# Modulation rows by matmuls of 32 columns, with the squares and scalings spread between them

## The chip, the cores and the metric

The kernel runs on one core of a Trainium2 chip. The metric is the device time of one execution in microseconds (us). The engines named below are PE (the matrix engine, TensorE), PEld (its weight loads, shown apart), DVE (VectorE), ACT (ScalarE), POOL (GpSimd) and SP (SyncE, which here issues the DMAs).

## The reference, cut to what matters

One layer of a diffusion backbone: a short gated convolution and a bidirectional mLSTM side by side, then a gated feed-forward network. There are 128 context tokens and 2048 latent tokens of width 1024, all in float32. The shift, scale and gate vectors of each normalisation come from a conditioning vector, one for the context and one for the latent tokens:

```python
mod_ctx = (jax.nn.silu(c_ctx) @ w_mod[l] + b_mod[l])[None, None, :]
mod_lat = (jax.nn.silu(c) @ w_mod[l] + b_mod[l])[:, None, :]
...
shift1, scale1, gate1, shift2, scale2, gate2 = jnp.split(mod, 6, axis=-1)
h = rmsnorm(x, norm1) * (1 + scale1) + shift1
z = h @ w_in                                    # conv parts, q, k, v, o, mLSTM gates
...
h_m, C, n, m = mlstm_bidir(heads(q), heads(k), heads(v), gates, C0, n0, m0)
...
x = x + gate1 * (jnp.concatenate([y_sc, h_m], axis=-1) @ w_out)
h2 = rmsnorm(x, norm2) * (1 + scale2) + shift2
up = conv3((h2 @ w_up).reshape(B, rows, row_len, 2 * D_FF), conv_ffn_w, conv_ffn_b, axis=ffn_axis)
a, gg = jnp.split(up.reshape(B, T, 2 * D_FF), 2, axis=-1)
x = x + gate2 * ((jax.nn.silu(gg) * a) @ w_down)
```

`mod` has 6 x 1024 entries for each of the two conditioning vectors. In blocks of 128 these are 48 modulation rows of the kernel (16 of them are `shift1` and `scale1`).

## The kernel before, in words

Tokens stand along the free axis, channels on the 128 partitions (8 tiles of 128 channels). Nothing can be multiplied by `w_in` before the input is normalised, scaled and shifted, so the kernel opens with the following, in `hymba_kernel`:

- `mod_pe(mt)` computes one modulation row. SP loads a tile of `w_mod` of 128 x 1024 (512 KB) into one of six buffers (`wsu` twice, `xg` four times, by `homes6`). Eight float32 matmuls (L628) accumulate over the 8 channel tiles. Their stationary operand is the weight block of 128 x 128; the moving operand `csil` has two distinct columns (context and latent), repeated by a broadcast to 128. DVE then adds the bias (L630) and writes the two columns that matter into `modT`.
- `mods(k0, k1)` runs rows 8+k (scale) and k (shift) for each k and then `affine` (L120), which makes the combined scale `ab`. The 16 rows are called w0 to w15 below, in this order.
- `gsquares` squares the 8 input tiles of the first 512 tokens on ACT and adds them on DVE (L590). `inv_rms` sums over partitions by four matmuls of one column (L129), scales on DVE (L132) and takes the power on POOL (L133). `spread` broadcasts the result to all partitions by four matmuls (L140).
- `gapply` multiplies each input tile (L600) and adds the shift; `put` (L594, L595) splits the result into a rounded high part `hH` and a low part `hL`. Float32 products are done as three matmuls of such parts.
- `vg_of(0)`, by `vg` (L397 to L404), then computes values and gates for the first block: 8 groups of 24 matmuls of 264 columns, each group ended by a write-out on ACT (L402) and an addition on DVE (L404). `second()` prepares the next block meanwhile.

The other 32 modulation rows aren't needed until late. `mod_dve` (the function around L896) computes them on DVE: for each row one load of 512 KB and two multiply-and-sum instructions over 128 x 1024 (half-rows). It is a generator called `side`. Its steps are called from three places: `vg_first` (values and gates of the blocks after those), the gate phase, and the weave of the mLSTM sums. The gate phase (`gate_phase`) computes the log forget gates on DVE and ACT (`fe`, `fc`), which PE transposes (L964).

The program is written through a scheduling layer that sets each engine's order from the order of the code, with its own view of costs and of free buffers; so an instruction may stand elsewhere on its engine than in the code.

Of the kernel before, what the change touches and what calls it, by code (L numbers as in the profile page):

```python
# [10 lines left out]
F32 = mybir.dt.float32  # L11
F32R = mybir.dt.float32r
AF = mybir.ActivationFunctionType
# [5 lines left out]
P = 128  # L19
# [24 lines left out]
def bc(ap, shape):  # L44
    return ap.to_broadcast(shape)
# [13 lines left out]
def hymba_kernel(ctx: ExitStack, tc: tile.TileContext, I, O):  # L59
    nc = tc.nc  # L60
    V, S, G, PE, Q = nc.vector, nc.scalar, nc.gpsimd, nc.tensor, nc.sync
# [30 lines left out]
    csil = cst.tile([P, KT, 2], F32, name="csil")  # L92
# [8 lines left out]
    ssp = ctx.enter_context(tc.tile_pool(name="ssp", bufs=2))  # L101

    def run(g, side=None, every=1):
        for i, _ in enumerate(g):
            if side and i % every == 0:
                next(side, None)
# [11 lines left out]
    def affine(n, k0, k1):  # L118
        s0 = 8 if n == 0 else 32
        V.scalar_tensor_tensor(ab[:, n, k0:k1], modT[:, s0 + k0:s0 + k1, :], 1.0,  # L120
                               bc(nrm[:, n, k0:k1, None], [P, k1 - k0, 2]), op0=ALU.add, op1=ALU.mult)

    def inv_rms(ss, n, r):

        nch = (n + P - 1) // P
        ps = pst.tile([P, 512], F32, name="st")
        for i in range(nch):
            w = min(P, n - i * P)
            PE.matmul(ps[:w, i:i + 1], ss[:, i * P:i * P + w], ones[:, 0:1], start=True, stop=True)  # L129
        for i0, i1, w in ((0, n // P, P), (n // P, nch, n % P)):  # L130
            if i0 < i1 and w:
                V.tensor_scalar(r[:w, i0:i1], ps[:w, i0:i1], 1.0 / D, EPS, op0=ALU.mult, op1=ALU.add)  # L132
                G.tensor_tensor(r[:w, i0:i1], r[:w, i0:i1], mhalf[:w, i0:i1], op=ALU.pow)  # L133

    def spread(r, n):

        ps = pst.tile([P, 512], F32, name="st")
        for i in range((n + P - 1) // P):
            w = min(P, n - i * P)
            PE.matmul(ps[:, i * P:i * P + w], bc(r[:w, i:i + 1], [w, P]), ident[:w, :w], start=True, stop=True)  # L140
        return ps
# [63 lines left out]
    def accumulator():  # L205
        pool = pa[next(turn_a) % len(pa)]
        return pool.tile([P, 512], F32, name="acc")
# [157 lines left out]
    with ExitStack() as ph1:  # L365
# [4 lines left out]
        sqp = ph1.enter_context(tc.tile_pool(name="sqp", bufs=2))  # L370
# [14 lines left out]
        def load_vg(j):  # L385
            return [load_w(I["w_vg"][j, kk], WN) for kk in range(2)]
# [163 lines left out]
        with tc.tile_pool(name="ex", bufs=1, side="right") as ex, \  # L550
# [16 lines left out]
            def raws(blk):  # L567
                def get(pool, name, k0, n, bufs):
                    t = pool.tile([P, 4, 384] if n > 2 else [P, 2, NG], F32, name=name, bufs=bufs)
                    t = t.rearrange("p k t -> p (k t)")[:, :n * NG].rearrange("p (k t) -> p k t", t=NG)  # L570
                    Q.dma_start(t, I["x"][k0:k0 + n, :, TG + blk * NG:TG + (blk + 1) * NG].rearrange("k p t -> p k t"))
                    return [t[:, i] for i in range(n)]

                if blk == 0:
                    return get(xp, "xt", 0, 3, 2) + get(xp, "xt", 3, 3, 2) + get(xg, "xh", 6, 2, 1)
                return [x for k in range(0, KT, 2) for x in get(xg, "xg", k, 2, 4)]

            def gcol(blk):
                c = TG // P + 4 * blk
                return rc[:, c:c + 4]  # L580

            def gsquares(xr):
                ss = ssp.tile([P, 512], F32, name="ss")
                for k, x in enumerate(xr):
                    if k == 0:
                        S.activation(ss, x, AF.Square)
                        continue
                    sq = sqp.tile([P, 512], F32, name="sq")
                    S.activation(sq, x, AF.Square)
                    V.tensor_add(ss, ss, sq)  # L590
                return ss

            def put(x, to):
                S.activation(to[0], x, AF.Copy)  # L594
                V.tensor_sub(to[1], x, to[0].bitcast(F32))  # L595

            def gapply(blk, xr):
                rb = spread(gcol(blk), NG)
                for k, x in enumerate(xr):
                    V.scalar_tensor_tensor(x, x, ab[:, 0, k, 1:2], rb[:, :NG], op0=ALU.mult, op1=ALU.mult)  # L600
                    S.activation(x, x, AF.Identity, bias=modT[:, k, 1:2])
                    put(x, plain[blk][k])
                    yield

            def gsums(x1, x2):
                for kk in range(4):
                    b11, b21, b12, b22 = x1[kk], x1[kk + 4], x2[kk], x2[kk + 4]
                    V.tensor_sub(b11, b12, b11)
                    put(b11, gs[0][kk])
                    V.tensor_sub(b12, b22, b12)  # L610
                    yield
                    V.tensor_sub(b22, b22, b11)
                    put(b22, gs[1][kk])
                    V.tensor_sub(b21, b21, b22)
                    put(b12, gs[2][kk])
                    yield
# [3 lines left out]
            def mod_pe(mt):  # L620
                if next(homes6) == "u":
                    st = ex.tile([P, WN], F32, name="wsu", bufs=2)
                else:
                    st = xg.tile([P, 2, NG], F32, name="xg", bufs=4).rearrange("p k t -> p (k t)")
                Q.dma_start(st[:, :D], I["w_mod"][mt])
                ps = accumulator()
                for k in range(KT):
                    PE.matmul(ps[:, :P], st[:, k * P:(k + 1) * P], bc(csil[:, k, None, :], [P, 64, 2]),  # L628
                              start=(k == 0), stop=(k == KT - 1))
                V.tensor_scalar(modT[:, mt, :], ps[:, :2], bmod[:, mt:mt + 1], None, op0=ALU.add)  # L630

            def mods(k0, k1):
                for k in range(k0, k1):
                    mod_pe(8 + k)
                    mod_pe(k)
                    affine(0, k, k + 1)
# [6 lines left out]
            Q.dma_start(ident, I["ident"])  # L643
            mods(1, 2)
            x1 = raws(0)
            ss = gsquares(x1)
            mods(2, 4)
            ws = load_vg(0)
            inv_rms(ss, NG, gcol(0))
            mods(4, 8)  # L650
            run(gapply(0, x1))
            ws += load_vg(1)
            Q.dma_start(bgate, I["b_gate"].to_broadcast([P, 16]))
            x2 = raws(1)

            def second():
                ss = gsquares(x2)
                yield
                inv_rms(ss, NG, gcol(1))
                yield  # L660
                yield from gapply(1, x2)
# [5 lines left out]
            side = second()  # L667
# [6 lines left out]
            side = gsums(x1, x2)  # L674
# [187 lines left out]
            side = chain(first_stats(), prep_down())  # L862
# [39 lines left out]
        side = mod_dve()  # L902
# [277 lines left out]
        def weave(units, fill, blocks, lead, side=None):  # L1180

            n = len(units)
            for i in range(-1, n + 3):
                if 0 <= i < n:
                    units[i].first()
                if 0 <= i - 3 < n:
                    units[i - 3].third()
                if 0 <= i - 1 < n:
                    units[i - 1].second()
                for x in range(lead) if i < 0 else (i + lead,):  # L1190
                    if x < n:
                        units[x].load()
                for _ in range(blocks[i % 3]):
                    next(fill, None)
                if side and i % 2:
                    next(side, None)


        def vg_first():
            for b in BA:  # L1200
                hH, hL = hs[b]
                yield from vg(chunks(b), lambda k: (hH[:, k], hL[:, k]), ws, rq)

        for x, _ in enumerate(vg_first()):
            next(third, None)
            if x % 2:
                next(side, None)
        run(third)
        with tc.tile_pool(name="gt", bufs=1, side="right") as gt:
            gph = gate_phase()  # L1210
            kh = heads(BA, hs, 16, kD, AF.Copy, 1.0)
            while True:
                try:
                    next(gph)
                except StopIteration as e:
                    cols, colc, decB = e.value
                    break
                run(islice(kh, 2), side, 2)
            run(kh, side, 2)
        sbs, sfs = [], []  # L1220
        for hp in range(2):
            sb = ml.tile([P, 2, 2, 129], F32, name="sb", bufs=5)
# [31 lines left out]
        side = sums(0, fpool, (0,), (6,))  # L1254
# [16 lines left out]
    with ph2:  # L1271
# [141 lines left out]
        side = sums(1, fpool)  # L1413
# [77 lines left out]
        for w, (hf, x) in enumerate(PRODS):  # L1491
            n = HN[hf] // 2 // NP[hf]
            for mp, ps in units_of(w):
                acc = {p: bank(next(turn))[:, :n] for p in ps}
                for c, nk in enumerate(KS):
# [4 lines left out]
                    for p in ps:  # L1500
                        for kk in range(nk):
                            k = slice(kk * P, (kk + 1) * P)
# [9 lines left out]
                    if jobs and jobs[0][0] + 1 <= step:  # L1512
                        k, ch = jobs[0]
# [93 lines left out]
```

## Time and profile before

| quantity | value |
|---|---|
| median of 3 runs | 2476.62 us (2476.61 to 2480.12) |
| the profiled execution, in all | 2481.01 us |
| its span in the profile | 2479.2 us |
| mean granted clock of PE | 0.991 |
| PE / PEld / DVE / ACT busy | 98% / 94% / 73% / 46% |
| PE's idle time before the first modulation row | 5.6 us |
| PE's idle time before the fifth row | 3.3 us |
| PE's idle time before the first matmul of `vg_of(0)` | 2.6 us |
| PE's idle time before L964 (gate phase) | 3.4 us |

Durations are read from the profiled execution and held against its own span; the median of the runs is what is compared between kernels. PE is busy nearly always, so the places that matter are those at which it stands idle or runs at a lower granted clock. The profile gives the granted clock for any stretch of time; a share of 0.50 means half of full speed.

### The profile page before, as it was taken

What the parts mean: (1) busy time and instruction counts of PE and PEld (TensorE: products, weight loads), DVE (VectorE), ACT (ScalarE), POOL (GpSimd) and SP (SyncE); (2) the same over time, 40 slices, a digit from 0 to 9 for tenths busy, and PEclk for the clock granted to TensorE, in tenths of its full rate; (3) what the DMA queues carried; (4) which work ended last, traced back from release to release, by engine and by line L of the source; (5) the groups of instructions that cost most, each with busy time, mean ns of one, the idle gap of its engine ahead of it and who ended that gap; (6) DMA issues with size and microseconds to landing.
All of it is one profiled execution on the core that took longest, in us unless ns stands there. A gap on an engine that the chain in (4) does not pass through costs nothing.

```text
span 2479.2 us, 42907 instructions
## 1 busy us (share of the span) xinstructions
PE 2427.5 (98%) x16347; PEld 2322.7 (94%) x16347; DVE 1806.6 (73%) x3419; ACT 1146.3 (46%) x2166; POOL 65.4 (3%) x127
## 2 busy tenths in 40 slices
PE   8999999999999999999999999999999999999998
PEld 7987889989999989999999999999999988889998
DVE  4767678862567776888798879776767787677665
ACT  4533453352344444465454446555545554543343
POOL 0000000000101110000000000000000000000000
PEclk9999999999999999999999999999999999999999
DMA  7457557787567886966465446544444486576444
GB/s 287 129 191 256 206 191 223 234 257 217 163 190 232 280 249 197 302 233 234 143 229 195 164 143 240 185 149 161 138 161 145 164 292 221 201 275 208 173 155 149
DMA packets 249119, 506.08 MB, mean 204 GB/s; under 512 B 22722, under 2 KB 143698, under 8 KB 238034
## 3 DMA queue, kind: packets, MB, share of 16 engines
q1 hardware_dynamic: 248914, 503.35, 61.0%
q8 instruction: 128, 2.10, 0.4%
q14 instruction: 77, 0.63, 0.1%
HBM read 355.24 MB, written 148.03 MB: 203 GB/s over the span
## 4 chain that ended last, share of the span: by engine, by line
PE 78%; DMA 11%; DVE 7%; issue 2%; ACT 1%; SPq 1%; POOL 0%; DVEq 0%; ACTq 0%; POOLq 0%
PE pa L1446 7%; PE pa L1448 7%; PE pa L1447 7%; PE acc L216 4%; PE acc L218 4%; PE acc L217 4%; PE pb L1448 3%; PE pb L1446 3%; PE pb L1447 3%; PE pa L1505 2%; PE pa L1504 2%; PE pa L1506 2%; PE pc L1446 2%; PE pc L1448 2%; PE pc L1447 2%; DMA wm<-in_w_modr 2%
## 5 line engine op out<-in xcount | busy, mean ns | idle before, releaser
L1446 PE MATMUL pa<-tH,wh 128*128 128x272 f32 x1408 | 409.1, 291 | 3.1 <-DVE row L502 2.3
L1448 PE MATMUL pa<-tH,wl 128*128 128x272 f32 x1408 | 408.3, 290 | 0.0
L1447 PE MATMUL pa<-tL,wh 128*128 128x272 f32 x1408 | 406.3, 289 | 0.3 <-DVE tL L283 0.3
L289 ACT ACTIVATE wh<-st 128x512 fp32r<-128x512 f32 (+1 forms) x312 | 189.5, 609 | 412.8 <-PE pa L1447 117.2
L216 PE MATMUL acc<-hH,wh 128*128 128x384 f32 (+1 forms) x960 | 330.4, 344 | 0.0
L218 PE MATMUL acc<-hH,wl 128*128 128x384 f32 (+1 forms) x960 | 322.0, 335 | 0.0
L217 PE MATMUL acc<-hL,wh 128*128 128x384 f32 (+1 forms) x960 | 321.2, 335 | 0.0
L1287 DVE SCALAR_TENSOR_TENSOR tt<-raw,fw,tt 128x127 f32<-128x127 f32 (+4 forms) x264 | 242.3, 948 | 43.5 <-ACT tt L1293 42.3
L290 DVE TENSOR_TENSOR wl<-st,wh 128x512 fp32r<-128x512 f32 (+1 forms) x312 | 205.4, 661 | 92.8 <-ACT wh L289 88.9
L1446 PEld LDWEIGHTS pa<-tH,wh 128*128 128x128 f32 x1408 | 265.9, 189 | 3.9 <-DVE row L502 2.4
L1447 PEld LDWEIGHTS pa<-tL,wh 128*128 128x128 f32 x1408 | 266.7, 189 | 0.5 <-DVE tL L283 0.5
L1448 PEld LDWEIGHTS pa<-tH,wl 128*128 128x128 f32 x1408 | 265.6, 189 | 0.0
L1446 PE MATMUL pb<-tH,wh 128*128 128x272 f32 x704 | 204.0, 290 | 1.9 <-ACT tH L282 1.1
L1448 PE MATMUL pb<-tH,wl 128*128 128x272 f32 x704 | 203.8, 290 | 0.0
L1447 PE MATMUL pb<-tL,wh 128*128 128x272 f32 x704 | 202.9, 288 | 0.0
L216 PEld LDWEIGHTS acc<-hH,wh 128*128 128x128 f32 x960 | 182.0, 190 | 1.4 <-issue 0.4
L217 PEld LDWEIGHTS acc<-hL,wh 128*128 128x128 f32 x960 | 181.7, 189 | 0.8
L218 PEld LDWEIGHTS acc<-hH,wl 128*128 128x128 f32 x960 | 181.5, 189 | 0.4 <-issue 0.2
L289 ACT ACTIVATE wh<-s 128x512 fp32r<-128x512 f32 x176 | 110.9, 630 | 150.5 <-PE pc L1447 90.5
L290 DVE TENSOR_TENSOR wl<-s,wh 128x512 fp32r<-128x512 f32 x176 | 120.8, 687 | 32.1 <-ACT wh L289 28.3
L1446 PEld LDWEIGHTS pb<-tH,wh 128*128 128x128 f32 x704 | 132.6, 188 | 2.5 <-ACT tH L282 1.3
L1447 PEld LDWEIGHTS pb<-tL,wh 128*128 128x128 f32 x704 | 132.9, 189 | 0.1
(301 smaller groups left out, 5931.9 us busy)
## 6 DMA issues: line engine op xcount, KB each, us to landing
st<-in_w_up SPq DMA_DIRECT2D x88, 512.0 KB, 4.7
wU<-s SPq DMA_DIRECT2D x22, 1024.0 KB, 7.6
s<-wU SPq DMA_DIRECT2D x22, 1024.0 KB, 5.5
st<-wD SPq DMA_DIRECT2D x32, 704.0 KB, 4.2
st<-in_w_down SPq DMA_DIRECT2D x28, 704.0 KB, 4.2
wst<-in_w_in SPq DMA_DIRECT2D x38, 512.0 KB, 4.6
R<-nD SPq DMA_DIRECT2D x34, 512.0 KB, 5.0
wm<-in_w_modr SPq DMA_DIRECT2D x32, 512.0 KB, 4.9
```

The costliest lines, as they stand in the source:

```text
L216: PE.matmul(acc[:, :n], w_h, hH[:, k, :n], start=(k == 0), stop=False)
L217: PE.matmul(acc[:, :n], w_h, hL[:, k, :n], start=False, stop=False)
L218: mm = PE.matmul(acc[:, :n], w_l, hH[:, k, :n], start=False, stop=(k == KT - 1))
L289: S.activation(wh[:, :n], a, AF.Copy)
L290: V.tensor_sub(wl[:, :n], a, wh[:, :n].bitcast(F32))
L1287: V.scalar_tensor_tensor(o, i, w, o, op0=ALU.mult, op1=ALU.add)
L1446: PE.matmul(acc, wh[:, w], rh, start=(kk == 0 and i in (0, 1, 5)), stop=False, skip_group_check=True)
L1447: PE.matmul(acc, wh[:, w], rl, start=False, stop=False, skip_group_check=True)
L1448: mm = PE.matmul(acc, wl[:, w], rh, start=False, stop=(kk == 3), skip_group_check=True)
L1504: PE.matmul(acc[p], wh[:, k], th[:, t], start=(c == kk == 0), stop=False, skip_group_check=True)
L1505: PE.matmul(acc[p], wh[:, k], tl[:, t], start=False, stop=False, skip_group_check=True)
L1506: PE.matmul(acc[p], wl[:, k], th[:, t], start=False, stop=(c == 2 and kk == nk - 1), skip_group_check=True)
```

## The change

The modulation rows by matmul get a moving operand of 32 columns instead of 128 (the two distinct columns repeated 16 times). The squares of the first block become a generator that is run three tiles at a time between row pairs 2, 3 and 4. Then follow the sum of squares, row pair 5, and the scaling, three tiles at a time between the pairs 6 and 7. The steps of the other modulation rows are moved: 7 in `vg_first` instead of 9, none in the gate phase, and three of four steps in the weave of the sums (`i % 4`) instead of every second.

```diff
-            def gsquares(xr):
-                ss = ssp.tile([P, 512], F32, name="ss")
+            def gsquares(xr, ss):
                 for k, x in enumerate(xr):
                     if k == 0:
                         S.activation(ss, x, AF.Square)
...
+                    yield
...
-                    PE.matmul(ps[:, :P], st[:, k * P:(k + 1) * P], bc(csil[:, k, None, :], [P, 64, 2]),
+                    PE.matmul(ps[:, :32], st[:, k * P:(k + 1) * P], bc(csil[:, k, None, :], [P, 16, 2]),
                               start=(k == 0), stop=(k == KT - 1))
...
             x1 = raws(0)
-            ss = gsquares(x1)
-            mods(2, 4)
+            ss = ssp.tile([P, 512], F32, name="ss")
+            sq = gsquares(x1, ss)
+            for k in range(2, 5):
+                mods(k, k + 1)
+                run(islice(sq, 3))
             ws = load_vg(0)
             inv_rms(ss, NG, gcol(0))
-            mods(4, 8)
-            run(gapply(0, x1))
+            mods(5, 6)
+            ap = gapply(0, x1)
+            for k in range(6, 8):
+                run(islice(ap, 3))
+                mods(k, k + 1)
+            run(ap)
             ws += load_vg(1)
...
-                if side and i % 2:
+                if side and i % 4:
                     next(side, None)
...
-            if x % 2:
+            if x < 14 and x % 2:
                 next(side, None)
...
-                run(islice(kh, 2), side, 2)
-            run(kh, side, 2)
+                run(islice(kh, 2))
+            run(kh)
```

In the following listings a row is an instruction with its line, output and inputs, and its tile; x16 stands for sixteen in a row. Below each other stand the kernel before and the changed one; in the latter the lines of `mod_pe` are L627 and L629 instead of L628 and L630, and those of the adds, the scaling and `mod_dve` have moved too. The first two are PE's from the start of the program up to the first matmuls of vg:

```order
L628 MATMUL acc<-csil,wsu 128x128 x16
L628 MATMUL acc<-csil,xg 128x128 x32
L628 MATMUL acc<-csil,wsu 128x128 x16
L129 MATMUL st<-ones,ss 128x1 x4
L628 MATMUL acc<-csil,xg 128x128 x32
L628 MATMUL acc<-csil,wsu 128x128 x16
L628 MATMUL acc<-csil,xg 128x128 x16
L140 MATMUL st<-ident,rc 128x128 x4
L397 MATMUL acc<-wh,hH 128x264
```

```order
L627 MATMUL acc<-csil,wsu 128x32 x16
L627 MATMUL acc<-csil,xg 128x32 x24
L129 MATMUL st<-ones,ss 128x1 x4
L627 MATMUL acc<-csil,xg 128x32 x8
L140 MATMUL st<-ident,rc 128x128 x2
L627 MATMUL acc<-csil,wsu 128x32 x8
L140 MATMUL st<-ident,rc 128x128 x2
L627 MATMUL acc<-csil,wsu 128x32 x8
L627 MATMUL acc<-csil,xg 128x32 x32
L627 MATMUL acc<-csil,wsu 128x32 x8
L397 MATMUL acc<-wh,hH 128x264
```

The sum of squares stands after five rows instead of eight, the spread in two halves around the seventh row instead of after all sixteen, and three rows stand among the matmuls of vg. The next two are DVE's from the first row's bias on:

```order
L630 TENSOR_SCALAR modT<-acc,bmod 128x2
L590 TENSOR_TENSOR ss<-ss,sq 128x512 x7
L630 TENSOR_SCALAR modT<-acc,bmod 128x2
L120 SCALAR_TENSOR_TENSOR ab<-modT,nrm 128x2
L630 TENSOR_SCALAR modT<-acc,bmod 128x2 x2
```

```order
L629 TENSOR_SCALAR modT<-acc,bmod 128x2
L589 TENSOR_TENSOR ss<-ss,sq 128x512 x7
L629 TENSOR_SCALAR modT<-acc,bmod 128x2
L132 TENSOR_SCALAR rc<-st 128x4
L120 SCALAR_TENSOR_TENSOR ab<-modT,nrm 128x2
L629 TENSOR_SCALAR modT<-acc,bmod 128x2 x2
L120 SCALAR_TENSOR_TENSOR ab<-modT,nrm 128x2
L599 SCALAR_TENSOR_TENSOR xt<-xt,ab,st 128x512 x2
```

The adds of the squares (L590, L589) follow the fourth row's bias in both; what stands behind them has changed. The last two are DVE's in the gate phase, around `fe` and `fc` (`wm` is a half-row of `mod_dve`):

```order
L950 COPY fc<-gates 128x64
L896 SCALAR_TENSOR_TENSOR wm,mt<-wm,cB 128x1024
L954 SCALAR_TENSOR_TENSOR fe<-fc 128x136
L896 SCALAR_TENSOR_TENSOR wm,mt<-wm,cB 128x1024
L115 TENSOR_TENSOR wl<-wst,wh 128x512
L897 TENSOR_SCALAR modT<-mt,bmod 128x2
L115 TENSOR_TENSOR wl<-wst,wh 128x512
L957 SCALAR_TENSOR_TENSOR fc<-fc,fe 128x136
```

```order
L957 COPY fc<-gates 128x64
L115 TENSOR_TENSOR wl<-wst,wh 128x512
L961 SCALAR_TENSOR_TENSOR fe<-fc 128x136
L115 TENSOR_TENSOR wl<-wst,wh 128x512
L903 SCALAR_TENSOR_TENSOR wm,mt<-wm,cB 128x1024
L904 TENSOR_SCALAR modT<-mt,bmod 128x2
L964 SCALAR_TENSOR_TENSOR fc<-fc,fe 128x136
```

Between `fc`'s copy and `fe` stands a piece of a weight split (L115) instead of a half-row, and one half-row instead of two before the last instruction.

More of the change, by code (lines that the diff above doesn't have):

```diff
@@ L586, in gsquares @@
                         S.activation(ss, x, AF.Square)
[L587 to L591, printed above, removed]
+                    else:
+                        sq = sqp.tile([P, 512], F32, name="sq")
+                        S.activation(sq, x, AF.Square)
+                        V.tensor_add(ss, ss, sq)
+                    yield
             def put(x, to):
@@ L656, in second @@
             def second():
-                ss = gsquares(x2)
+                ss = ssp.tile([P, 512], F32, name="ss")
+                run(gsquares(x2, ss))
                 yield
```

## Prediction

> **What bounds the kernel now.** I read the head of the page first, to see which engine sets the span:
>
> ```profile
> span 2479.2 us, 42907 instructions
> PE 2427.5 (98%) x16347; PEld 2322.7 (94%) x16347; DVE 1806.6 (73%) x3419; ACT 1146.3 (46%) x2166; POOL 65.4 (3%) x127
> ```
>
> TensorE (PE) is busy for 98% of the span. So an edit counts only where it changes how long PE works or stands idle. The list of waits says where PE stands idle and which of those places the change touches:
>
> ```profile
> PE acc L628 <- DMA wsu<-in_w_mod: 5.6, 1, 5.6
> PE S L964 <- DVE fc L957: 3.4, 1, 3.4
> PE acc L628 <- DVE ss L590: 3.3, 1, 3.3
> PE acc L397 <- ACT hH L594: 2.6, 1, 2.6
> ```
>
> Three of them lie in the first 46 us (the first weight, the squares, the scaled input), one in the gate stage. I then read the timeline of PE from the start (start, duration, what ran, in brackets the idle time before it). A modulation row is 16 records, since each float32 matmul shows as two:
>
> ```profile
> 5.61 5.19 PE L628 MATMUL acc<-csil,wsu 128*128 128x128 f32 x32 [5.61 <-DMA wsu<-in_w_mod]
> 10.63 3.73 PE L628 MATMUL acc<-csil,xg 128*128 128x128 f32 x32
> 17.64 5.44 PE L628 MATMUL acc<-csil,xg 128*128 128x128 f32 x32 [3.27 <-DVE ss L590]
> 22.91 3.73 PE L628 MATMUL acc<-csil,wsu 128*128 128x128 f32 x32
> 26.48 0.95 PE L129 MATMUL st<-ones,ss 128*128 128x1 f32 x8
> 27.29 7.39 PE L628 MATMUL acc<-csil,xg 128*128 128x128 f32 x64
> 34.52 3.73 PE L628 MATMUL acc<-csil,wsu 128*128 128x128 f32 x32
> 41.67 1.05 PE L140 MATMUL st<-ident,rc 128*128 128x128 f32 x8
> 45.36 0.39 PE L397 MATMUL acc<-wh,hH 128*128 128x264 f32 x1 [2.63 <-ACT hH L594]
> ```
>
> At full clock four rows take 34.52 - 27.29 = 7.23 us, 1.81 us each (0.113 a record). The first two took 10.63 - 5.61 = 5.02 us; with the second at 1.8, the first took about 3.4 us, 0.213 a record, twice as long. The last row of the listing starts the gate and value matmuls (here "vg") of the first block.
>
> **What 32 columns cost at full clock.** The trace has the extreme case of narrow matmuls, the one-column sums of squares, seen on the weight loads (PEld) and once while the clock was low:
>
> ```profile
> 26.37 0.97 PEld L129 LDWEIGHTS st<-ones,ss 128*128 128x128 f32 x8
> 27.27 0.86 PEld L628 LDWEIGHTS acc<-csil,xg 128*128 128x128 f32 x7
> ...
> 900.37 1.44 PE L129 MATMUL st<-ones,ss 128*128 128x1 f32 x6 [4.63 <-DVE o L1175]
> 901.67 0.56 PE L1121 MATMUL S<-q,k 128*128 128x128 f32 x1
> ```
>
> Eight one-column records took 27.27 - 26.37 = 0.90 us, 0.113 each: exactly what 128 columns take. A row is bound by its 16 weight loads, and 32 columns save nothing while the clock is full. With the clock low six took 1.30 us, 0.217 each. So a row of 32 columns costs 1.8 us warm and 3.41 us (16 x 0.213) cold; the edit's own gain is zero. The Trainium skill, "TensorE: Matmul & The Clock Gate", section "LDWEIGHTS (loading the stationary operand)", prices a load at P/1.2 ns, 107 ns for 128, with no word of the array's clock. By that the cold row would be 1.7 us, and the whole cold case below would shrink to that of rival A; the 0.217 us of this trace is against it.
>
> **What 32 columns do to the clock.** The view by windows gives busy time of PE, PEld, DVE, ACT, POOL, then the granted clock, for stretches of 3.41 us on the grid on which the clock is seen to change:
>
> ```profile
> 5.07:8.48 3.41, 2.87 (x13) 2.90 (x14) 0.00 (x0) 0.00 (x0) 0.00 (x0) 1.00 0.97 318
> 15.31:18.72 3.41, 1.08 (x10) 1.11 (x11) 2.98 (x5) 2.75 (x5) 0.00 (x0) 1.00 1.02 409
> 18.72:22.13 3.41, 3.41 (x19) 3.41 (x18) 1.56 (x4) 0.35 (x1) 0.00 (x0) 0.50 1.03 419
> 530.72:534.13 3.41, 1.57 (x10) 1.17 (x9) 1.30 (x3) 3.15 (x10) 0.00 (x0) 1.00 0.63 200
> 534.13:537.55 3.42, 3.42 (x21) 3.29 (x20) 2.93 (x7) 1.21 (x5) 0.00 (x0) 1.00 0.96 296
> 2404.64:2408.06 3.42, 2.60 (x20) 2.21 (x18) 0.83 (x3) 0.63 (x1) 1.66 (x2) 1.00 0.00 0
> 2408.06:2411.47 3.41, 3.41 (x16) 3.37 (x16) 1.88 (x4) 0.00 (x0) 0.00 (x0) 0.50 0.25 87
> ```
>
> (In the first of them the column says 1.00 though the pitch is that of the half clock until 8.48.) After a stretch with 1.08 us of PE work the clock falls to half for the next stretch. But 1.57 us at 530 kept it, and 2.60 us at 2404 lost it. So busy time isn't what is counted, and weight loads aren't either (2.21 against 1.17). What differs is the width, in the groups of those two stretches:
>
> ```profile
> L129 PE MATMUL st<-ones,ss 128*128 128x1 f32 x4 | 0.5, 229 | 0.0
> L1074 PE MATMUL y<-vw,kT 128*128 128x258 f32 x4 | 1.2, 382 | 0.0
> ```
>
> At 2404 eight of the 20 records are one or 32 columns wide, at 530 all are 128 to 384. My reading, an inference from few stretches: the clock follows the columns streamed. In shares of what a full clock could stream I get, by adding records times columns, about 0.40 for 2404 (lost) and 0.44 for 530 (kept), so a limit near 0.41. A 128-column row streams nearly all of its time: 0.95 warm, 0.5 cold, and the clock rose at 8.48. A 32-column row has a quarter of that: 0.24 warm, 0.12 cold. By this the clock never rises during the rows.
>
> **The change, part by part, in that cold case** (PE's order as the listings of the change show it).
> - Rows w0 to w3: from 5.61, 4 x 3.41, to 19.25. w4 follows at once, to 22.66; its weight had landed by 17.64.
> - Squares: DVE's adds follow the fourth drain in both kernels:
>
> ```profile
> 14.41 0.22 DVE L630 TENSOR_SCALAR modT<-acc,bmod 128x2 f32<-128x2 f32 x1 [1.37 <-PE acc L628]
> 14.54 5.46 DVE L590 TENSOR_TENSOR ss<-ss,sq 128x512 f32<-128x512 f32 x7
> ```
>
>  That drain moves from 14.41 to about 19.4, so the adds end at 25.0 (19.4 + 0.13 + 5.46) and PE, whose next work is now the sum of squares, is idle for 2.4 us. Sum 1.7 us (8 x 0.217) to 26.8, w5 to 30.2; POOL's power for the scale lies beside w5.
> - Spread in two halves (2 x 0.85) with w6 between, then w7 to w12: 7 x 3.41 + 1.7 = 25.6, to 55.8. The scaling on DVE and ACT (each 0.7 us a tile) goes beside it; the 2.63 us wait before L397 goes, since the scaling starts some 20 us before vg. Weights for vg are asked for after two more row loads on SP's queue; vg starts 10 us later than before, so that costs nothing, unless rows run warm, when it is 2 x 0.5 MB, 2.5 us at the 409 GB/s above.
> - 23 vg records stand between w12 and the end of w15. Their pitch and the end of block 0, its eighth write-out, are these:
>
> ```profile
> 46.52 0.42 PE L398 MATMUL acc<-wl,hH 128*128 128x264 f32 x1
> 46.74 1.08 PE L399 MATMUL acc<-wh,hL 128*128 128x264 f32 x4
> 54.03 0.29 PE L397 MATMUL acc<-wh,hH 128*128 128x264 f32 x1
> 54.16 0.28 PE L398 MATMUL acc<-wl,hH 128*128 128x264 f32 x1
> 75.58 0.36 ACT L402 ACTIVATE rv<-acc 128x256 f32<-128x256 f32 x1
> ```
>
>  Cold 0.22, warm 0.12 to 0.13. So 23 x 0.22 + 3 x 3.41 = 15.3, to 71.1. Then the clock needs one whole stretch of vg, some 23 records cold (5.1), and the last 146 of 192 run at 0.121 (17.7), with the second block's sums and spread (0.95 + 1.05, as above) among them: the end is at 95.8, against 75.6. **+20.2 us.** Bounds: if a mixed stretch of nine vg records and a row lifts the clock already, w14, w15 and the vg behind them go at double speed, 6 to 10 us less (+10); if other waits join, +24.
> - Gate stage: PE waits there for `fc`:
>
> ```profile
> 404.53 1.22 DVE L896 SCALAR_TENSOR_TENSOR wm<-wm,cB 128x1024 f32<-128x1024 f32 x1
> 407.19 1.28 ACT L956 ACT_TABLE_LOAD   x1
> 408.83 0.30 DVE L957 SCALAR_TENSOR_TENSOR fc<-fc,fe 128x136 f32<-128x136 f32 x1 [1.75 <-ACT fe L956]
> 409.19 0.47 PE L964 MATMUL S<-ident,fc 128*128 128x128 f32 x1 [3.39 <-DVE fc L957]
> ```
>
>  Fewer modulation half-rows of 1.22 us stand on DVE ahead of `fc`: 20 instead of 22, not none, since the order still fills DVE with them. One of them stood directly between the gates and `fe`; its 1.2 us goes, and a table load and ACT remain in the wait. I take -1.5; the bounds are -5.5 (3.39 of wait and half of a stretch at half clock go) and, with three of four steps instead of one in two carrying a half-row pair in the next stage, +2, where DVE at 73% has room.
>
> Sum: +20.2 - 1.5 = +18.7 on 2479.2, a span of 2497.9. The profiled execution took 2481.0 in all, 4.4 above the median of 2476.6; taken off that median, 2476.6 + 18.7 = **2495 us**. The case's own range is 2484 to 2503.
>
> **Rivals.**
> - A, faster: the clock rises as before, because weight loads or any matmul count as work. For it: in the first stretch the clock rose after 2.87 us of busy time, and no stretch of the trace is filled with narrow rows alone. Against it: the stretch at 2404. Then rows take 1.81; w4 still waits for its weight until 17.64 and the sums for DVE until 20.1, w5 to w12 end at about 38, the 23 vg records and w13 to w15 at 46.2, and the other 169 at 0.121 and 2.0 for the second block's sums end at 68.7: -6.9, with the gates -8.4, **2468**. It decides if a row counts for more than about 0.41. The Trainium skill, same page, section "What's actually happening", says that what is issued in the first 3.4 us runs at 1.2 GHz and all after it at 2.4, with a window that runs freely; the grid above agrees with the window, and the first half of the sentence would give this rival. Chance 0.19.
> - B, within the noise: the clock flips, rising after the spreads (128 columns) and in half of the rows. Half of 20 is +10, less the gates and a larger part of the waits removed: **2480**, if it rises early. Against it: two spreads of four records are 1.7 us in 5. Chance 0.08.
> - C: narrow rows run faster than the one-column sums did, and the loads of 0.5 MB at 409 GB/s (1.28 us) bound the start: 16 rows and 2 MB of input end at about 31, vg at 38, and block 0 at about 61: **2460**. The 0.113 above speaks against it. Chance 0.03. The Trainium skill, same page, section "Wait — 56ns, not 53.3ns?", gives a floor of 25 ns between narrow matmuls, which no row here shows with a new weight for each.
>
> **How the numbers follow.** The cold case has 0.70. A measurement of this kernel tells 0.2%, 5 us, from no change: 2471.7 to 2481.6 counts as same. Faster: A, C and little of B, 0.22. Same: most of B, 0.06. Slower: the cold case and the rest, 0.72. The range reaches from A, 2467, to the end of the cold case, 2503; C and longer stalls stay out.
>
> **What would show it.** In the timeline the rows w1 to w12 have 0.213 a record and the windows from 8.48 on show half clock (right), or 0.113 (A); the sums of squares at 25 to 27 or at 20; vg begins at 56 or 38; the eighth write-out of L402 at 96 or 69. PE's wait before L964 should be 2.2 us or less. What would make the forecast wrong above all is that weight loads count for the clock after all: I infer the opposite from two stretches.

## The result, and the profile after

The changed kernel took 2499.06 us (median; 2498.19 to 2501.3), the kernel before 2476.62 us: a ratio of 1.0089, 95% interval 1.0076 to 1.0103. That is 22.4 us slower; forecast were 18.7 us, 2495 us in all. The profiled execution of the changed kernel took 2498.82 us, its span is 2497.0 us.

PE's timeline from the start, in the columns of before:

```profile
5.72 7.01 PE L627 MATMUL acc<-csil,wsu 128*128 128x32 f32 x32 [5.72 <-DMA wsu<-in_w_mod]
12.54 10.43 PE L627 MATMUL acc<-csil,xg 128*128 128x32 f32 x48
25.24 1.86 PE L129 MATMUL st<-ones,ss 128*128 128x1 f32 x8 [2.27 <-DVE ss L589]
26.96 3.60 PE L627 MATMUL acc<-csil,xg 128*128 128x32 f32 x16
30.38 1.20 PE L140 MATMUL st<-ident,rc 128*128 128x128 f32 x4
31.37 3.46 PE L627 MATMUL acc<-csil,wsu 128*128 128x32 f32 x16
34.64 1.20 PE L140 MATMUL st<-ident,rc 128*128 128x128 f32 x4
38.91 13.84 PE L627 MATMUL acc<-csil,xg 128*128 128x32 f32 x64
...
56.57 0.56 PE L397 MATMUL acc<-wh,hH 128*128 128x264 f32 x1 [0.40 <-DVE modT L629]
75.31 0.42 PE L399 MATMUL acc<-wh,hL 128*128 128x264 f32 x1
75.53 0.34 PE L397 MATMUL acc<-wh,hH 128*128 128x264 f32 x1
75.70 0.28 PE L398 MATMUL acc<-wl,hH 128*128 128x264 f32 x1
```

Four rows now take 52.56 - 38.91 = 13.65 us (the fifth begins at 52.56), 0.213 us a record; before, four took 7.23 us. The clock rises only at about 75.5, where the distance between vg records falls from 0.22 to 0.12 us. The eighth write-out of the first block comes at 97.93 us instead of 75.58:

```profile
97.93 0.37 ACT L402 ACTIVATE rv<-acc 128x256 f32<-128x256 f32 x1
```

That is a lag of 22.35 us, and it is still 22.5 us on POOL at 163.38 us (185.88 in the changed kernel). The gate phase gives some of it back. These are PE's last row ahead of its transposes and its last row before the next group of transposes, in the kernel before and then in the changed one:

```profile
405.46 0.34 PE L218 MATMUL acc<-hH,wl 128*128 128x384 f32 x1
420.29 0.34 PE L218 MATMUL acc<-hH,wl 128*128 128x384 f32 x1
```

```profile
427.60 0.34 PE L218 MATMUL acc<-hH,wl 128*128 128x384 f32 x1
427.78 0.31 PE L971 MATMUL S<-ident,fc 128*128 128x128 f32 x1
430.62 0.47 PE L971 MATMUL S<-ident,ic 128*128 128x128 f32 x1 [2.02 <-DVE ls L972]
440.03 0.34 PE L218 MATMUL acc<-hH,wl 128*128 128x384 f32 x1
```

The lag goes from 22.14 to 19.74 us, so the gate phase gives back 2.4 us. The 3.39 us ahead of the first of the two transposes are gone and 2.02 us stand ahead of the second; half clock follows for one stretch of 3.41 us instead of two.

Behind the gate phase the lag wanders. It is 17.5 us at 546 us of the kernel before and 21.2 us at 562, where PE waits longer in the changed kernel and its clock falls to half for a stretch (567.19 to 570.60 of its own time), which it doesn't in the kernel before. It is 21.25 us at the first rows of the head normalisation (633.84 and 655.09), and the two spans end 17.8 us apart, in a pair of which the execution before was 4.4 us above its median. So it is in part chance that the medians differ by the same 22.4 us as the start does.

### The profile page after: what moved, and what is told of

It is laid out like the page before. It is cut to its first block, busy times and chain, and to the rows that moved or that the text cites. A ratio compares the mean times of both kernels' runs of the same rounds, so it can differ in the third digit from the quotient of the medians.

```text
span 2497.0 us, 42903 instructions
## 1 busy us (share of the span) xinstructions
PE 2451.0 (98%) x16347; PEld 2348.2 (94%) x16347; DVE 1808.3 (72%) x3419; ACT 1153.0 (46%) x2170; POOL 65.8 (3%) x127
## 4 chain that ended last, share of the span: by engine, by line
PE 80%; DMA 9%; DVE 6%; issue 1%; ACT 1%; SPq 1%; POOL 0%; DVEq 0%; ACTq 0%; POOLq 0%
PE pa L1453 7%; PE pa L1455 7%; PE pa L1454 7%; PE acc L216 4%; PE acc L218 4%; PE acc L217 4%; PE pb L1455 4%; PE pb L1453 3%; PE pb L1454 3%; PE pa L1511 2%; PE pa L1512 2%; PE pa L1513 2%; PE acc L627 2%; PE pc L1454 2%; PE pc L1455 2%; PE pc L1453 2%
```

## The experiments

Each was compared with runs of the kernel before on the same chip (medians 2474.1 to 2475.1 us there).

### The width alone

```diff
-PE.matmul(ps[:, :P], st[...], bc(csil[:, k, None, :], [P, 64, 2]), ...)
+PE.matmul(ps[:, :32], st[...], bc(csil[:, k, None, :], [P, 16, 2]), ...)
```

> The kernel before with 32 instead of 128 columns in the modulation rows, and nothing else. Theory (narrow rows leave the clock low; the order of the code hardly counts): the start goes as in the changed kernel, rows at 0.213 us a record, eighth write-out at about 98 us, and only the gain in the gate stage (1.25 us, 22.5 against 21.25 us of lag) is missing: 2476.6 + 22.4 + 1.3 = about 2500 us, 2496 to 2504. Rival (the spreading of squares and scalings between the rows costs the time, by DVE's adds or the new order): below 2482 us, rows at 0.113.

Measured: 2501.78 us, ratio 1.0113 (1.0087 to 1.0140). The start of this kernel:

```profile
5.59 7.01 PE L628 MATMUL acc<-csil,wsu 128*128 128x32 f32 x32 [5.59 <-DMA wsu<-in_w_mod]
25.11 1.86 PE L129 MATMUL st<-ones,ss 128*128 128x1 f32 x8 [2.27 <-DVE ss L590]
56.45 0.56 PE L397 MATMUL acc<-wh,hH 128*128 128x264 f32 x1 [0.40 <-DVE modT L630]
```

They are the rows of the changed kernel, 0.12 to 0.13 us earlier, the sum of squares after five rows included. So the narrow width alone makes the whole loss, and it makes the new order at the start of PE too: the scheduling layer places the sum and the spread there as in the changed kernel, though the code is written as before. The interval of the ratio (21 to 35 us) holds the changed kernel's 22.4 as well. (The 1.25 us of this expectation and the next two is what the lag loses between 163 and 634 us, not what the gate phase alone gives back.)

### Everything but the width

```diff
-PE.matmul(ps[:, :32], ..., bc(csil[:, k, None, :], [P, 16, 2]), ...)
+PE.matmul(ps[:, :128], ..., bc(csil[:, k, None, :], [P, 64, 2]), ...)
```

> The changed kernel with 128 columns in the rows again, all else as changed. Theory: rows at 0.113 us a record from the second on, all 16 done at about 42 us, the 2.63 us wait before the first vg matmul gone (the scaling starts earlier), gate stage 1.25 us shorter: 2476.6 - 2.6 - 1.3 = about 2473 us, 2469 to 2476. Rival (the spreading costs): 2485 us or more.

Measured: 2471.18 us, ratio 0.9983 (0.9971 to 0.9995): faster than the kernel before. Its start:

```profile
5.59 5.41 PE L627 MATMUL acc<-csil,wsu 128*128 128x128 f32 x32 [5.59 <-DMA wsu<-in_w_mod]
26.75 3.73 PE L627 MATMUL acc<-csil,xg 128*128 128x128 f32 x32
30.33 0.95 PE L129 MATMUL st<-ones,ss 128*128 128x1 f32 x8
42.75 0.37 PE L397 MATMUL acc<-wh,hH 128*128 128x264 f32 x1
```

The first vg record is at 42.75 without a wait, against 45.36 after 2.63 us of waiting. In the windows of this kernel the stretch from 63.09, at half clock before, isn't slow any more:

```profile
63.09:66.51 3.42, 3.42 (x31) 3.42 (x30) 3.42 (x8) 3.42 (x7) 0.10 (x1) 1.00 0.14 46
```

31 records instead of 18 fit into it. So the rest of the change is worth some 3.5 us (2474.7 less 2471.2, on one chip), and the width costs about 26 us, with the 22.4 of the changed kernel added. At the eighth write-out, 70.28 here against 97.93, it is 27.65 us. The width changes the order too: with 128 columns the sum of squares stands after ten rows, with 32 after five.

### The moved steps of the other rows alone

```diff
-                if side and i % 2:
+                if side and i % 4:
...
-            if x % 2:
+            if x < 14 and x % 2:
...
-            run(kh, side, 2)
+            run(kh)
```

> The kernel before with only the moved steps of the other modulation rows (7 in the first values, none in the gate phase, three of four in the weave). Theory: the start is unchanged, the gate stage 1.25 us shorter: about 2475.4 us, 2472 to 2477. Rival (the half-rows moved to the weave delay something there): 2478 us or more.

Measured: 2472.17 us, ratio 0.9989 (0.9973 to 1.0005). The interval takes in no change, so the time alone decides nothing. The trace shows what the changed kernel's does, the wait at the second transpose instead of the first:

```profile
407.72 0.33 PE L964 MATMUL S<-ident,fc 128*128 128x128 f32 x1
410.58 0.33 PE L964 MATMUL S<-ident,ic 128*128 128x128 f32 x1 [2.01 <-DVE ls L965]
```

### The spreading alone, with 128 columns

The kernel of the second experiment, with the three places of the third as they were before.

> The changed kernel with 128 columns and the steps of the other modulation rows where they were before: the spreading of squares and scalings alone. Theory: the wait before the first vg matmul (2.63 us) goes, all else stays: about 2474 us, 2471 to 2476.5. Rival (the spreading itself costs, since sums and scalings now wait for DVE among the rows): 2480 us or more.

Measured: 2470.97 us, ratio 0.9987 (0.9972 to 1.0001), not told apart from no change by the time alone (and 0.03 us below the expected range). The wait before vg is gone here too; the 3.25 us ahead of the first transpose are still there:

```profile
42.10 0.37 PE L397 MATMUL acc<-wh,hH 128*128 128x264 f32 x1
402.08 0.33 PE L971 MATMUL S<-ident,fc 128*128 128x128 f32 x1 [3.25 <-DVE fc L964]
```

The rival, that the spreading itself costs 3 us or more, is excluded.

### 64, 96 and 80 columns: where the clock rises

These three are the changed kernel with another width in the same line (`[P, 32, 2]`, `[P, 48, 2]`, `[P, 40, 2]`).

> The changed kernel with 64 columns in the rows. Reading of the prediction (the clock follows the columns streamed, limit near 0.41 of a full clock): 64 columns stream 0.25 while the clock is low, so it never rises in the rows; 0.213 us a record, about 2499 us, 2494 to 2504. Rival (the limit lies on the width of a matmul, below 64, or on matmul time): rows at 0.113, about 2472 us.

> The changed kernel with 96 columns. Reading of the prediction: 96 columns stream 0.375 while the clock is low, below 0.41: rows at 0.213, about 2499 us. Rival (what counts is the share of the array's own cycles at the clock it has, 0.75 here, while the stretch that was kept low in the trace had at most 0.6): the clock rises after the first stretch, rows at 0.113, about 2472 us. Either limits the threshold from one side.

> The changed kernel with 80 columns: 0.62 of the array's own cycles while the clock is low, between 64 columns (0.5, stayed low) and 96 (0.75, rose). If the limit lies at 0.6 or below, the clock rises in the first rows and the time is about 2472 us; if it lies above, rows at 0.213 and about 2493 to 2497 us, a little less for less of vg at low clock.

Measured: 64 columns 2493.43 us, ratio 1.0068 (1.0047 to 1.0088); 80 columns 2494.58, 1.0077 (1.0050 to 1.0104); 96 columns 2472.31, 0.9989 (0.9970 to 1.0009). The 64-column kernel came out 0.6 us below its expected range, the 80-column kernel within it. Rows of PE's timeline from each, 64, 80 and 96 in turn:

```profile
12.13 13.86 PE L627 MATMUL acc<-csil,xg 128*128 128x64 f32 x64
```

```profile
12.11 13.86 PE L627 MATMUL acc<-csil,xg 128*128 128x80 f32 x64
```

```profile
11.96 3.74 PE L627 MATMUL acc<-csil,xg 128*128 128x96 f32 x32
17.54 5.41 PE L627 MATMUL acc<-csil,xg 128*128 128x96 f32 x32 [1.84 <-DMA xg<-in_w_mod]
22.78 3.74 PE L627 MATMUL acc<-csil,wsu 128*128 128x96 f32 x32
```

64 and 80 columns stay at half clock (0.213 us a record, 64 records in 13.65 us); 96 go to full clock, fall after the wait for the fifth row's weight, rise again, and fall once more at 32.1 us, in a wait of 1.75 us. The step is sharp: between 80 and 96 columns lie 22 us. The forecast for 96 was wrong: it put the limit at 0.41 of what a full clock can stream, and 96 columns at the low clock stream 0.375 and raised it.

The prediction had that limit from two stretches; the twelve traces hold 8704 of them, and counting them all gives another value. A 264-column record of vg takes 0.22 us at half clock, so a full clock streams about 2.4 such columns a nanosecond; float32 records of 512 columns take 0.43 us each at full clock (eight in 18.83 - 15.39 us, in the last experiment), 1.2 columns a nanosecond.

With these rates I added up, for each stretch of the grid, the time that its columns need at full clock; streaming is taken to begin 0.07 us after a record's start, the value that fits best, and the start of a program counts as half clock, as the distance between its records shows. Behind a stretch with less than 0.375 of a full clock's columns the next one is at half clock, behind one with more it is at full clock, whichever clock the stretch itself had: 77 fell and 8397 stayed at full clock, 77 rose and 153 stayed at half. Only stretches within 0.015 of the limit are ever on the wrong side of it, three of them at most. Busy time of PE puts 91 stretches on the wrong side and busy time of the weight loads 103, even with a limit of its own for each direction.

So the columns streamed in a stretch decide, with one limit near 0.375. In shares of the cycles that the array has at its own clock this looks like two limits: 0.75 to rise (80 columns have 0.62, 96 have 0.75) and 0.375 to fall. The two stretches of the prediction come out at 0.375 (lost, 2404) and 0.381 (kept, 530) in this count, not at 0.40 and 0.44.

### 128 columns in two rows, then 64

```diff
+n = 128 if mt in (0, 8) else 64
...
+PE.matmul(ps[:, :n], ..., bc(csil[:, k, None, :], [P, n // 2, 2]), ...)
```

> The changed kernel with 128 columns in the first two rows and 64 in the other 14. Reading of the prediction: the first two rows raise the clock, 64 columns at full clock stream 0.48, above 0.41, and keep it up as long as PE doesn't wait; the wait for the fifth row's weight may drop it (it did before, at 18.72 us), and then 64 columns can't raise it again: rows w1 to w3 at 0.113, rows after the wait at 0.213 until vg, about 2490 us, 2482 to 2496. Rival (only the width counts): rows at 0.213 from the third row on, about 2496 us; or all at 0.113, 2472 us.

Measured: 2490.92 us, ratio 1.0067 (1.0043 to 1.0091).

```profile
5.79 6.63 PE L628 MATMUL acc<-csil,wsu 128*128 128x128 f32 x32 [5.79 <-DMA wsu<-in_w_mod]
12.25 3.68 PE L628 MATMUL acc<-csil,xg 128*128 128x64 f32 x32
17.69 6.30 PE L628 MATMUL acc<-csil,xg 128*128 128x64 f32 x32 [1.76 <-DVE ss L589]
37.55 10.34 PE L628 MATMUL acc<-csil,xg 128*128 128x64 f32 x48
```

The same 64-column rows run at 0.11 us a record from 12.25 on, and at 0.21 (48 in 10.13 us) from 37.55 on, where the profile gives 0.50 for the clock; between lies the wait at 17.69. So 64 columns are enough to keep the clock (about 0.5 of a full clock's columns at 0.11 us a record) and too few to raise it (0.25), and the width isn't a limit by itself.

### 32 columns with filling

Eighteen matmuls of ones by ones into the row's own accumulator, overwritten by the row, are added; they compute nothing of the result.

```diff
+for _ in range(3 if mt == 8 else 1):
+    PE.matmul(ps, ones, bc(ones[:, None, :], [P, 4, P]), start=True, stop=True)
 for k in range(KT):
     PE.matmul(ps[:, :32], ...)
```

> The changed kernel, 32 columns, with one idle float32 matmul of 512 columns (ones by ones, overwritten) ahead of each row and two more ahead of the first: 18 that compute nothing of use, each 0.85 us at full clock, 15.4 us of extra work. Theory (the low clock is the whole loss): the filling raises the share streamed to about 0.48 and the clock rises before the second row; rows at 0.113, eighth write-out at about 75 to 80 us instead of 98, total 2475 to 2482 us, faster than without the extra work. Rival (narrow rows are slow in themselves, or the order costs the time): 2510 us or more.

Measured: 2506.15 us, ratio 1.0130 (1.0110 to 1.0150): the expected range was missed by 24 us, and the interval (2502 to 2512 us) reaches the rival's 2510, so the time alone doesn't decide against the rival. The timeline does:

```profile
1.04 5.49 PE L627 MATMUL acc<-ones 128*128 128x512 f32 x6 [1.04 <-DVE mhalf L91]
16.35 1.87 PE L629 MATMUL acc<-csil,xg 128*128 128x32 f32 x16
18.05 1.96 PE L627 MATMUL acc<-ones 128*128 128x512 f32 x4
19.85 1.87 PE L629 MATMUL acc<-csil,xg 128*128 128x32 f32 x16
23.91 1.66 PE L129 MATMUL st<-ones,ss 128*128 128x1 f32 x8 [2.19 <-DVE ss L589]
25.43 2.06 PE L627 MATMUL acc<-ones 128*128 128x512 f32 x2
27.27 3.46 PE L629 MATMUL acc<-csil,xg 128*128 128x32 f32 x16
```

Among the filling a row of 32 columns takes 18.05 - 16.35 = 1.70 us, at full clock. Then PE waits 2.19 us for the squares and sums them by one-column matmuls; behind that a row takes 30.55 - 27.27 = 3.28 us (the next begins at 30.55), about twice as long. The windows give the granted clock (the third number from the end) around the first and in the second:

```profile
17.38:20.79 3.41, 3.41 (x22) 2.45 (x21) 2.22 (x5) 1.35 (x3) 0.00 (x0) 1.00 1.02 413
27.62:31.03 3.41, 3.41 (x18) 3.41 (x17) 0.22 (x1) 0.00 (x0) 0.00 (x0) 0.50 0.01 4
```

The first half of the theory is shown within one kernel: narrow rows aren't slow in themselves, 1.70 us against 3.28. The expectation left out that a wait drops the clock and that the same filling, spread over twice the time, doesn't raise it again.

### 128 columns, with the wait filled

```diff
+if mt == 1:                       # behind the fourth row
+    ps = accumulator()
+    for _ in range(4):
+        PE.matmul(ps, st[:, :P], bc(ones[:, None, :], [P, 4, P]), start=True, stop=True)
```

> The changed kernel with 128 columns, and four float32 matmuls of 512 columns (the fourth row's weight by ones, overwritten) behind the fourth row, 3.4 us at full clock, in the time in which PE waits for the fifth row's weight. Theory: the wait no longer drops the clock, the stretch of half clock behind it (two rows in 5.27 us instead of 3.6) goes, the first vg matmul starts about 1.7 us earlier than in the kernel with 128 columns alone (42.75), at about 41: total about 2469.5 us, 2466 to 2473. Rival (the clock falls at another place instead, in the sum of squares or the wait for the spread, or the filling delays the fifth row): first vg at 42.5 or later, 2471 us or more.

Measured: 2469.51 us, ratio 0.9973 (0.9962 to 0.9985). It is the fastest median of the study and clearly faster than before; against the second experiment's 2471.18 (0.9971 to 0.9995) the intervals overlap, so it isn't shown to beat that.

```profile
15.39 3.60 PE L633 MATMUL acc<-ones,xg 128*128 128x512 f32 x8
18.83 3.73 PE L627 MATMUL acc<-csil,xg 128*128 128x128 f32 x32
32.24 1.22 PE L140 MATMUL st<-ident,rc 128*128 128x128 f32 x4 [1.75 <-POOL rc L133]
33.26 4.67 PE L627 MATMUL acc<-csil,xg 128*128 128x128 f32 x32
45.28 0.37 PE L397 MATMUL acc<-wh,hH 128*128 128x264 f32 x1
```

The filled wait does keep the clock: two rows take 3.57 us behind it, not 5.27. But the scheduling layer put the spread right behind the sum, and PE waits 1.75 us there and falls for a while (4.51 us for two rows). The first vg record is at 45.28, where the rival had it, and the eighth write-out at 72.89 comes 2.6 us later than the 70.28 of the second experiment. The total agrees with the expectation, the step to it doesn't; that agreement is luck, and why the total is low all the same stays open.

## Why the prediction was right

- **Width at full clock.** "32 columns save nothing": shown, but for 0.1 us a row. The one-column rows had given 0.113 us a record; a 32-column row among filling takes 1.70 us, 0.107 a record, the 128-column row 1.8.
- **The clock never rises during the rows.** Shown, in the changed kernel and with the width alone. The times by step: sum of squares forecast at 25.1, measured 25.24; idle time 2.4 and 2.27; vg at 55.8 and 56.57; the eighth write-out at 95.8 and 97.93.
- **The size.** The term of the start was too small by 2.15 us (20.2 against 22.35). 0.8 us are lost before vg, of which 0.40 is a wait for DVE's drain and 0.11 a later first weight. The clock then rises at 75.5 instead of 76.2, after about 40 records of vg and not 46, which makes up for them. So the 2 us are lost behind the rise: 0.76 us is the wait for POOL before the second block's spread, for which the sum had nothing (the kernel before has it too, 0.74 us), and the rest stays open:

```profile
87.84 1.16 PE L140 MATMUL st<-ident,rc 128*128 128x128 f32 x8 [0.76 <-POOL rv L401]
```

- **The gate stage.** -1.5 forecast, -2.4 measured across the gate phase: of the 3.39 us of waiting 2.02 came back at the second transpose, which the sum didn't name, and a stretch at half clock went, which it had only in its bound of -5.5. Later waits and falls of the clock move the lag by more than this term, and the sum had none of them.
- **The reason for it.** Columns streamed, not busy time nor weight loads, with one limit for rising and falling: shown, by all stretches of the twelve traces. The size of the limit was wrong. The stretches at 2404 and 530 don't have the 0.40 and 0.44 that the prediction gives them but 0.375 and 0.381, and the limit is near 0.375, not 0.41. That the two told the direction at all was luck, since they differ by less than 0.01. The size decided nothing here, because rows of 32 columns at the low clock stream 0.125; it did decide for 96 columns.
- **Rival A** (the clock rises as before, 2468 us) is what the kernel does at 96 and 128 columns: 2472.3 and 2471.2 us. It needs the streamed columns. The Trainium skill, "TensorE: Matmul & The Clock Gate", section "What's actually happening", lets everything behind the first 3.4 us of issued work run at full clock. Here PE worked from 25.24 to 75.5 us with one break, of 0.40 us, and stayed at half clock, so work that is issued isn't enough. The Trainium skill, same page, section "LDWEIGHTS (loading the stationary operand)", gives 107 ns for a load of 128 columns, with no word of the clock. The rows at half clock need 0.213 us a record, each with a load.

## What to carry to other kernels

The float32 matmuls of this kernel, each with a new weight, got hardly faster from fewer columns (0.107 us a record at 32, 0.113 at 128), but the columns are what keeps the clock up: 96 or more were needed to raise it and 64 could only hold it. Compare the distance between records, not the busy share, before and after such a cut. And where a scheduling layer sets the order, a cheaper-looking instruction moves others too, so test a new width alone and the new order alone before judging either.

## What the hardware showed that I had not expected

The granted clock in the profile doesn't show a clock that was low from the start. The same stretch, in the changed kernel and then in the one before:

```profile
8.48:11.90 3.42, 3.42 (x18) 3.42 (x18) 0.38 (x2) 0.00 (x0) 0.00 (x0) 1.00 1.01 390
```

```profile
8.48:11.90 3.42, 3.42 (x33) 3.42 (x32) 0.60 (x3) 0.00 (x0) 0.00 (x0) 1.00 1.03 404
```

18 records against 33 in the same time, and 1.00 in both. The mean clock of the slower kernel is even the higher one (0.993 against 0.991), for the changed kernel's 70 us at half clock don't appear in it, while the short falls after a rise do. And one count, the columns streamed in a stretch of 3.41 us, decides both ways, with one limit near 0.375 of what a full clock could stream. At half clock the same rows stream half as much, so 64 columns hold a clock that they can't raise.
